# A two-layer encoder trunk on one core: all eight pairs of an MLP part in seven-product form, GpSimd on half of the first product's lower parts, three raw buffers, new token places

## The chip, the cores and the metric

The kernel runs on one core of a Trainium2 chip. A core has a matrix engine (TensorE, PE in the profile, whose weight loads are listed apart as PEld), VectorE (DVE), ScalarE (ACT), GpSimd (POOL) and SyncE (SP, which here only issues transfers). Matmuls write to PSUM; everything else lies in SBUF. The metric is the device time of one execution in microseconds. The kernel before takes 1935.81 us (median of 3 runs, 1935.69 to 1936.0).

## The reference

The input is 256 tokens of width 2048, float32. Layer 0 mixes tokens with a convolution module, layer 1 with multi-head latent attention; each is followed by an MLP with a hidden width of 8192. The MLP is what the change is about:

```python
def sq_relu_mlp(h, w1, w2):
    return jnp.square(jax.nn.relu(h @ w1)) @ w2

for layer in range(DEPTH):
    h = rms_norm(x, norm_mixer_g[layer])
    x = x + (conv_module(h, ...) if layer % N_MIXERS == 0 else mla(h, ...))
    h = rms_norm(x, norm_mlp_g[layer])
    x = x + sq_relu_mlp(h, mlp_w1[layer], mlp_w2[layer])
return rms_norm(x, final_norm_g)
```

`w1` is 2048 x 8192 and `w2` 8192 x 2048 in each layer, 64 MB apiece.

## The kernel before, in words

**Float32 products from parts.** Each float32 operand is split into a higher part `hi` (a rounded copy, made by ScalarE) and a lower part `lo` (the operand minus `hi`, made by VectorE). A product takes three matmuls: hi·hi, lo·hi, hi·lo (`mm3`). The splitting of the weights runs on ScalarE and VectorE all along the kernel, since every weight is used once. `split_into` is the helper of the MLP: one ScalarE copy, then one VectorE subtraction whose two inputs, the raw weights and `hi`, both lie in SBUF.

**The MLP.** The hidden width is cut into 4 parts (q = 0 to 3) of 8 pairs (p = 0 to 7) of 128-wide blocks. The first product ("up", `up_units`) of a pair is made by two units; each loads 1 MB of `w1`, splits it in two halves (h = 0 and 1: one chunk each), and runs 16 matmuls of 512 columns and 16 of 256 columns against the tokens `xt`. After a pair's second unit a list of small steps follows: `add`, `square`, `forms`, `part` (the last splits the hidden values into `sh` and `sl`).

The second product ("down", `down_units`) of a pair with one half of the output width (n2 = 0 or 1) loads 1 MB of `w2`. It comes in two kinds. A plain unit has two chunks of 1024 columns and 24 matmuls of 512 columns. A seven-product unit treats the 2 x 2 blocks of the product in a Strassen-like way: sums of weight blocks (`T`, `V`) are made by VectorE first, four chunks are split (`one` with 512 columns, `two`, `t13` and `t24` with 1024), and 21 matmuls do. It also needs sums of hidden blocks (`forms`). In parts 0 to 2, seven of the eight pairs are of the second kind and pair 2 is plain; in part 3, three pairs (layer 0) or two (layer 1).

**The order of the work** is written out by `stream`. Part 0's up units run alone; then the down units of part q are interleaved with the up units of part q + 1 by the string `ORDERS` (S a seven-product unit, T an up unit, O the plain unit); part 3's down units run alone. So each layer has a first-product stage, three mixed windows and a second-product stage. `stream` splits the weights of the chunk that comes five places later before it issues the matmuls of a chunk (`WB` = 6 buffers of `hi` and of `lo`), and puts one or two of the waiting small steps ahead of each split. Raw weights go through three buffers of the pool `wpool` and a fourth in the MLP's own pool; a buffer is loaded again, by SyncE, once its last reader is done. Hidden values lie in 9 large slots (`N_S`) and 2 smaller ones (`N_G`).

**GpSimd** makes lower parts in the convolution stage (line 171 with the argument `nc.gpsimd`), works on the rotary keys in the attention stage (lines 1267 to 1272 and 1478), and does nothing in the MLPs.

**Places.** Pads of some 32-byte steps (`PAD_O`, `LO_GAP` and others) set where tiles lie. In the up product the lower parts begin 224 bytes into their buffers, so that they lie at 32 bytes modulo 64, while the tokens and `hi` lie at 0 modulo 64.

Of the kernel before, what the change touches and what calls it, by code (L numbers as in the profile page):

```python
# [10 lines left out]
F32 = mybir.dt.float32  # L11
# [7 lines left out]
P = 128  # L19
# [21 lines left out]
LO_GAP = 64  # L41
PAD_STATS = 48
PAD_O = 64
# [13 lines left out]
MADE = tuple((range(8),) * 3 + (last,) for last in ((0, 2, 1, 3, 4, 5, 6, 7),) * 2)  # L57
LATE_G = ((3, 5, 6, 7), (3, 4, 5, 6, 7))
# [25 lines left out]
def trunk_kernel(  # L84
# [231 lines left out]
    def open_xt(name):  # L316
        pool = right_pool(name, 1)
        xt[:] = [
            pool.tile([P, KC // NNB, 2 * S], F32R, name=nm("xt")) for _ in range(NNB)
        ]  # L320

# [3 lines left out]
    open_xt("xt0")  # L325
# [98 lines left out]
    def split_into(parts, src):  # L424
        nc.scalar.activation(parts[0], src, AF.Copy)  # L425
        nc.vector.tensor_tensor(parts[1], src, parts[0].bitcast(F32), op=ALU.subtract)  # L426

    def stream(chunks, todo, blocked, pool):
# [50 lines left out]
    def mlp(layer, ssq, next_gain, finish=None, before=None, last_w1=None):  # L479
# [3 lines left out]
        made_stage, pre, first_tiles, blocked, n_s, sums_left = [], [], {}, {}, [0], []  # L483
# [7 lines left out]
        def up_units(hs, q, p, extra):  # L491
# [3 lines left out]
            large = p in sevens or (q == PARTS - 1 and p in LATE_G[layer])  # L495

            def up_unit(b):
                ps = []

                def chunk(h):  # L500
                    def prep(raw, parts):
                        parts[h] = [a.rearrange("p a (j n) -> p (a j) n", n=P) for a in hi_lo(2, LO_GAP - 8)]
                        split_into(parts[h], raw[:, 8 * h : 8 * h + 8, :])
# [20 lines left out]
                    return Chunk(prep, run, [add, lambda: None, square, forms, part] + extra if b == 1 else [], now=out)  # L524
# [9 lines left out]
            def square():  # L534
                n_s[0] += large
                v = held["u"][:, :, :S]
                nc.scalar.activation(v, v, AF.Relu)
                if p in sevens:
                    held["f"] = f = f_tile()
                    nc.scalar.activation(f[:, 0:4, :].rearrange("p (b t) n -> p b (t n)", b=2), v, AF.Square)  # L540
                    held["src"], shape, tag, n = f[:, 1:8, :], [P, 7, P], "s", N_S
                else:
                    nc.scalar.activation(v, v, AF.Square)
                    held["src"], shape = v, [P, 2, S]
                    tag, n = ("s", N_S) if large else ("g", N_G)
                held["hl"] = [mp.tile(shape, F32R, tag=tag + c, name=nm(tag + c), bufs=n) for c in "hl"]

            def forms():
                if p in sevens:
                    f = held["f"]  # L550
                    nc.vector.tensor_tensor(
                        f[:, 4:6, :], f[:, 0:1, :].broadcast_to([P, 2, P]), f[:, 1:3, :], op=ALU.subtract
                    )
                    nc.vector.tensor_tensor(f[:, 6, :], f[:, 1, :], f[:, 5, :], op=ALU.subtract)
                    nc.vector.tensor_tensor(f[:, 7, :], f[:, 3, :], f[:, 6, :], op=ALU.subtract)

            def part():
                hs[p] = held["hl"]
                split_into(hs[p], held["src"])

            if large:
                blocked[square] = lambda: n_s[0] < N_S and not (p in sevens and sums_left)
            return [up_unit(b) for b in range(2)]

        def down_units(hs, q, n2, held, final):
# [3 lines left out]
            last_plain = max(p for p in range(NPAIR) if p not in sevens)  # L569
# [101 lines left out]
            def seven_unit(p):  # L671
# [80 lines left out]
        with ExitStack() as cx:  # L752
# [46 lines left out]
    with ExitStack() as cx:  # L799
# [389 lines left out]

        ssq, add, prepare = residual_stage(True, g_mlp[0])  # L1190
# [64 lines left out]
    with ExitStack() as cx:  # L1255
# [95 lines left out]

        kvh = at.tile([P, KR // P, S], F32R, name="kvh")
# [435 lines left out]
```

## Time and profile before

| what | value |
|---|---|
| median of 3 runs | 1935.81 us |
| the profiled execution | 1935.74 us |
| its span, first to last instruction | 1933.9 us |
| PE busy | 1910.2 us |
| DVE busy | 1651.6 us |
| ACT busy | 1204.9 us |
| POOL busy | 224.0 us |

Where the stages lie in the span of the profiled execution:

| stage | from | to |
|---|---|---|
| convolution module | 12 | 320 |
| MLP 0: part 0's up units alone | 321 | 409 |
| MLP 0: three mixed windows | 409 | 907 |
| MLP 0: part 3's down units alone | 907 | 982 |
| latent attention | 983 | 1253 |
| MLP 1: up units alone | 1254 | 1342 |
| MLP 1: three mixed windows | 1342 | 1841 |
| MLP 1: down units alone, final norm, output | 1841 | 1934 |

A row of instructions gives the line, the engine, the operation, the tiles written and read, the shape and the count; then busy time, the mean length of one in ns, and the engine's idle time ahead of them. In a row of the timeline the first two numbers are the start and the length in us. Neighbouring instructions of one engine overlap a little in the records (the next begins before the last has ended), so what an instruction costs its engine is the distance from its start to the next start.

### The profile page before, as it was taken

How to read it: one execution, taken by the hardware profiler on the slowest of the kernel's cores; microseconds unless marked ns; L12 is line 12 of the kernel's file. 1: busy time of each engine (PE TensorE's matmuls, PEld its weight loads, DVE VectorE, ACT ScalarE, POOL GpSimd, SP SyncE). 2: the span in 40 equal slices, each digit the busy share in tenths (PEclk: the TensorE clock that was granted, in tenths of full speed). 3: DMA queues.
4: the chain of work that ended last, by engine and by line, in shares of the span. 5: the costliest groups of instructions: out<-in, count | busy, mean ns of one | idle time of the engine just before them, and what ended most of it. 6: DMA issues, size and time to landing. Idle time of an engine off the chain costs nothing.

```text
span 1933.9 us, 28479 instructions
## 1 busy us (share of the span) xinstructions
PE 1910.2 (99%) x10778; PEld 1676.2 (87%) x10778; DVE 1651.6 (85%) x2374; ACT 1204.9 (62%) x1709; POOL 224.0 (12%) x183
## 2 busy tenths in 40 slices
PE   7999999999999999999999999999999999999998
PEld 7999888888888888888899998888888888888886
DVE  5999875789999999999976665657999999999887
ACT  5556664766666666666566665556766666666654
POOL 5999400000000000000001410000000000000000
PEclk9999999999999999999999999999999999999999
DMA  8666456857666667666646445765667766766663
GB/s 235 185 176 176 141 186 174 220 172 208 197 207 204 205 199 212 202 198 215 198 143 181 123 152 175 198 184 174 203 190 210 214 196 195 214 202 197 211 222 109
DMA packets 407113, 367.62 MB, mean 190 GB/s; under 512 B 15416, under 2 KB 351936, under 8 KB 406720
## 3 DMA queue, kind: packets, MB, share of 16 engines
q1 hardware_dynamic: 405952, 363.63, 63.0%
q10 hardware_dynamic: 1024, 2.17, 0.3%
q8 instruction: 84, 1.38, 0.3%
q14 instruction: 53, 0.43, 0.1%
HBM read 363.68 MB, written 2.10 MB: 189 GB/s over the span
## 4 chain that ended last, share of the span: by engine, by line
PE 98%; DVE 1%; DMA 1%; ACT 0%; issue 0%; DVEq 0%; ACTq 0%
PE acc L515 24%; PE acc L196 15%; PE acc L197 15%; PE acc L198 15%; PE acc L513 12%; PE acc L859 3%; PE acc L858 3%; PE acc L860 3%; PE acc L252 1%; PE sum L908 1%; PE acc L1443 0%; PE acc L1445 0%; PE acc L1444 0%; PE acc L1420 0%; PE acc L1421 0%; PE acc L1422 0%
## 5 line engine op out<-in xcount | busy, mean ns | idle before, releaser
L426 DVE TENSOR_TENSOR lo<-raw,hi 128x1024 fp32r<-128x1024 f32 (+1 forms) x512 | 571.8, 1124 | 88.0 <-ACT hi L425 87.7
L425 ACT ACTIVATE hi<-raw 128x1024 fp32r<-128x1024 f32 (+1 forms) x512 | 480.0, 971 | 66.0 <-PE acc L197 65.8
L515 PE MATMUL acc<-xt,hi 128*128 128x512 f32 x2048 | 504.0, 391 | 0.0
L515 PEld LDWEIGHTS acc<-xt,hi 128*128 128x128 f32 x2048 | 374.9, 188 | 72.6
L196 PE MATMUL acc<-hi,sh 128*128 128x512 f32 x930 | 362.7, 390 | 0.0
L198 PE MATMUL acc<-lo,sh 128*128 128x512 f32 x930 | 361.9, 389 | 0.0
L197 PE MATMUL acc<-hi,sl 128*128 128x512 f32 x802 | 312.0, 389 | 0.0
L513 PEld LDWEIGHTS acc<-xt,lo 128*128 128x128 f32 x2048 | 257.7, 188 | 10.9
L513 PE MATMUL acc<-xt,lo 128*128 128x256 f32 x2048 | 259.8, 279 | 0.0
L170 ACT ACTIVATE hi<-raw 128x1024 fp32r<-128x1024 f32 (+2 forms) x184 | 180.0, 1006 | 47.0 <-PE acc L197 42.9
L198 PEld LDWEIGHTS acc<-lo,sh 128*128 128x128 f32 x930 | 174.6, 188 | 36.3
L196 PEld LDWEIGHTS acc<-hi,sh 128*128 128x128 f32 x930 | 174.6, 188 | 35.9
L171 DVE TENSOR_TENSOR lo<-raw,hi 128x1024 fp32r<-128x1024 f32 (+2 forms) x118 | 132.9, 1147 | 68.6 <-ACT hi L170 63.0
L425 ACT ACTIVATE hi<-V 128x1024 fp32r<-128x1024 f32 x94 | 99.6, 1060 | 130.7 <-DVE V L721 123.6
L197 PEld LDWEIGHTS acc<-hi,sl 128*128 128x128 f32 x802 | 150.6, 188 | 31.1
L960 DVE SCALAR_TENSOR_TENSOR sum<-ub,w_dw,sum 128x256 f32<-128x256 f32 x400 | 163.5, 488 | 8.7 <-ACT sum L916 7.0
L171 POOL TENSOR_TENSOR lo<-raw,hi 128x1024 fp32r<-128x1024 f32 x66 | 157.8, 2413 | 24.5 <-ACT hi L170 24.5
L425 ACT ACTIVATE hi<-T 128x1024 fp32r<-128x1024 f32 x94 | 99.5, 1058 | 92.5 <-DVE T L709 69.0
L858 PE MATMUL acc<-xt,hi 128*128 128x256 f32 x512 | 146.3, 286 | 0.0
L859 PE MATMUL acc<-xt,hi 128*128 128x256 f32 x512 | 145.0, 283 | 0.5 <-DVE xt L209 0.5
L860 PE MATMUL acc<-xt,lo 128*128 128x256 f32 x512 | 144.9, 283 | 0.0
L520 ACT ACTIVATE U<-acc 128x512 f32<-128x512 f32 x128 | 75.8, 592 | 108.7 <-PE acc L515 108.6
(270 smaller groups left out, 2808.9 us busy)
## 6 DMA issues: line engine op xcount, KB each, us to landing
raw<-in_mlp_w SPq DMA_DIRECT2D x256, 1024.0 KB, 6.2
raw<-in_conv_w_pw SPq DMA_DIRECT2D x64, 512.0 KB, 5.6
raw<-in_conv_w_pw SPq DMA_DIRECT2D x16, 1024.0 KB, 5.1
raw<-in_mla_w_o SPq DMA_DIRECT2D x16, 1024.0 KB, 5.3
raw<-in_mla_w_kv_up SPq DMA_DIRECT2D x8, 1024.0 KB, 5.4
raw<-in_mla_w_in SPq DMA_DIRECT2D x8, 576.0 KB, 3.8
raw<-in_mla_w_in SPq DMA_DIRECT2D x4, 1024.0 KB, 7.4
raw<-in_mla_w_q_up SPq DMA_DIRECT2D x16, 256.0 KB, 5.0
```

Source lines behind the costliest of these rows:

```text
L170: nc.scalar.activation(hi, raw[:, js, :], AF.Copy)
L171: eng.tensor_tensor(lo, raw[:, js, :], hi.bitcast(F32), op=ALU.subtract)
L196: nc.tensor.matmul(ps, sh, mh, start=start, stop=False)
L197: nc.tensor.matmul(ps, sl, mh, start=False, stop=False)
L198: nc.tensor.matmul(ps, sh, ml, start=False, stop=stop)
L425: nc.scalar.activation(parts[0], src, AF.Copy)
L426: nc.vector.tensor_tensor(parts[1], src, parts[0].bitcast(F32), op=ALU.subtract)
L513: nc.tensor.matmul(ps[0][:, :S], wl[:, j, :], xh(k), start=False, stop=False)
L515: nc.tensor.matmul(ps[0], wh[:, j, :], xhl(k), start=k == 0, stop=k == KC - 1)
L858: nc.tensor.matmul(o, wh[:, bs], xh(k), start=k == 0, stop=False)
L859: nc.tensor.matmul(o, wh[:, bs], xl(k), start=False, stop=False)
L860: nc.tensor.matmul(o, wl[:, bs], xh(k), start=False, stop=k == KC - 1)
```

## The change

Parts 0 to 2 have all eight pairs in seven-product form, so pair 2's plain unit (and the letter O) is gone there; part 3 is as before. In the mixed windows the first half of an order has seven T and the second nine, where there were eight and eight. The hidden values have 11 slots of one size, in the room of the fourth raw buffer and of the two smaller slots. From part 1 on, the lower parts of the second half (h = 1) of each up unit are made by GpSimd. `forms` is cut into three steps (`forms`, `form_2`, `form_4`), which stand only after seven-product pairs. The step `norm`, in part 0, follows pair 2 and no longer the last pair. The tokens of the convolution stage lie 224 bytes lower (at 32 modulo 64), and move to their old place after it; the latents of the attention stage (`kvh` to `qpB`) lie 32 bytes higher.

The diff, without the parts that only move names:

```diff
+PAD_XT = 56
+PAD_KV = 8
-PAD_O = 64
+PAD_O = 56
...
-ORDERS = "STSTSTOSTSTSTSTT", "TSTSTSTOSTSTSTST"
-N_S, N_G = 9, 2
-SEVENS = tuple(((0, 1, 3, 4, 5, 6, 7),) * 3 + (last,) for last in ((0, 2, 4), (0, 2)))
...
+ORDERS = "STSTSTSSTSTSSTT", "TSTSTSTSTSTSTSTST"
+N_S = 11
+SEVENS = tuple((tuple(range(8)),) * 3 + (last,) for last in ((0, 2, 4), (0, 2)))
...
-    def split_into(parts, src):
+    def split_into(parts, src, eng=nc.vector):
         nc.scalar.activation(parts[0], src, AF.Copy)
-        nc.vector.tensor_tensor(parts[1], src, parts[0].bitcast(F32), op=ALU.subtract)
+        eng.tensor_tensor(parts[1], src, parts[0].bitcast(F32), op=ALU.subtract)
...
-        for home in (None, None, None, pool):
+        for home in (None, None, None):
             start(home)
...
-                for _ in range(2 if len(todo) > 4 else 1):
+                for _ in range(2 if len(todo) > 3 else 1):
...
-                        split_into(parts[h], raw[:, 8 * h : 8 * h + 8, :])
+                        split_into(parts[h], raw[:, 8 * h : 8 * h + 8, :], nc.gpsimd if h and q else nc.vector)
...
-                    return Chunk(prep, run, [add, lambda: None, square, forms, part] + extra if b == 1 else [], now=out)
+                    steps = [add, lambda: None, square, *([forms, form_2, form_4] if p in sevens else []), part]
+                    return Chunk(prep, run, steps + extra if b == 1 else [], now=out)
...
-            if large:
-                blocked[square] = lambda: n_s[0] < N_S and not (p in sevens and sums_left)
+            blocked[square] = lambda: n_s[0] < N_S and not (p in sevens and sums_left)
...
                 def close_one():
+                    while forms_left:
+                        todo.pop(0)()
...
-                    for unit in up_units(hs, q, p, [end] if p == MADE[layer][q][-1] and end is not None else [])
+                    for unit in up_units(hs, q, p, [end] if p == (2 if q == 0 else MADE[layer][q][-1]) and end is not None else [])
...
+        open_xt("xt0")
         ssq, add, prepare = residual_stage(True, g_mlp[0])
...
+        at.tile([P, PAD_KV], F32, name="pad_kv")
```

What moves is best seen on two engines. VectorE in layer 0's first mixed window, around the down unit of pair 2 (`lo<-raw` is the lower part of raw weights, with 1024 columns in the up units and in chunk `two`; `T` and `V` are sums of weight blocks, `W` sums of hidden blocks, `sl` the lower part of hidden values), before:

```order
L426 TENSOR_TENSOR lo_4888<-raw_4708,hi_4887 128x1024
L532 TENSOR_TENSOR U_4818<-U_4818 128x2x256
L426 TENSOR_TENSOR lo_4910<-raw_4708,hi_4909 128x1024
L426 TENSOR_TENSOR lo_4924<-raw_4740,hi_4923 128x1024
L551 TENSOR_TENSOR W_4919<-W_4919 128x256
L554 TENSOR_TENSOR W_4919<-W_4919 128x128
L555 TENSOR_TENSOR W_4919<-W_4919 128x128
L426 TENSOR_TENSOR lo_4937<-raw_4740,hi_4936 128x1024
```

An up unit gives two lower parts here (both from `raw_4708`), and the plain unit two (both from `raw_4740`). The same place on VectorE now:

```order
L429 TENSOR_TENSOR lo_4810<-raw_4630,hi_4809 128x1024
L719 TENSOR_TENSOR T_4835<-raw_4731 128x1024
L429 TENSOR_TENSOR lo_4844<-raw_4731,hi_4843 128x512
L726 TENSOR_TENSOR V_4836<-T_4835,raw_4731 128x512
L429 TENSOR_TENSOR lo_4855<-raw_4731,hi_4854 128x1024
L731 TENSOR_TENSOR V_4836<-V_4836,raw_4731 128x512
L429 TENSOR_TENSOR lo_4868<-T_4835,hi_4867 128x1024
L429 TENSOR_TENSOR lo_4878<-V_4836,hi_4877 128x1024
L429 TENSOR_TENSOR lo_4899<-raw_4762,hi_4898 128x1024
```

The up unit on `raw_4630` leaves one lower part on VectorE, and pair 2's unit on `raw_4731` has become a seven-product unit with seven VectorE instructions. GpSimd, from the end of the convolution module on (`lo` at line 171 are its lower parts, `m` and `pad_o` belong to the attention stage), before:

```order
L936 TENSOR_TENSOR tp_2965<-tp_2965,tp_2969 128x256
L171 TENSOR_TENSOR lo_2977<-raw_2632,hi_2976 128x1024
L171 TENSOR_TENSOR lo_2981<-raw_2758,hi_2980 128x1024
L1374 MEMSET pad_o 128x64
L1267 TENSOR_TENSOR m_10690<-scratch,cos 128x128
```

Nothing of layer 0's MLP stands between the convolution and the attention stage there. GpSimd from the same place on, now:

```order
L946 TENSOR_TENSOR tp_2966<-tp_2966,tp_2970 128x256
L172 TENSOR_TENSOR lo_2978<-raw_2633,hi_2977 128x1024
L172 TENSOR_TENSOR lo_2982<-raw_2759,hi_2981 128x1024
L429 TENSOR_TENSOR lo_4725<-raw_4525,hi_4724 128x1024
L429 TENSOR_TENSOR lo_4832<-raw_4630,hi_4831 128x1024
L429 TENSOR_TENSOR lo_4921<-raw_4762,hi_4920 128x1024
L429 TENSOR_TENSOR lo_5064<-raw_4927,hi_5063 128x1024
```

Between the same two stages 48 lower parts have been added, 16 in each mixed window (four are shown; the one on `raw_4630` is the second half of the up unit shown above), and 48 more in layer 1. Over the whole program VectorE's lower parts of 1024 columns from raw weights go from 512 to 404, GpSimd's from 66 to 162, and TensorE's matmuls of 512 columns fall by 36 (3 in each of 12 units).

More of the change, by code (lines that the diff above doesn't have):

```diff
@@ L53 @@
 FILL_AT = (5, 15)
-ORDERS = "STSTSTOSTSTSTSTT", "TSTSTSTOSTSTSTST"
-N_S, N_G = 9, 2
-SEVENS = tuple(((0, 1, 3, 4, 5, 6, 7),) * 3 + (last,) for last in ((0, 2, 4), (0, 2)))
-MADE = tuple((range(8),) * 3 + (last,) for last in ((0, 2, 1, 3, 4, 5, 6, 7),) * 2)
-LATE_G = ((3, 5, 6, 7), (3, 4, 5, 6, 7))
+ORDERS = "STSTSTSSTSTSSTT", "TSTSTSTSTSTSTSTST"
+N_S = 11
+SEVENS = tuple((tuple(range(8)),) * 3 + (last,) for last in ((0, 2, 4), (0, 2)))
+MADE = tuple((range(8),) * 3 + (last,) for last in ((0, 2, 1, 3, 4, 5, 6, 7), (0, 2, 1, 3, 4, 5, 6, 7)))
 N_WARM = 14
@@ L494, in up_units @@
             held = {}
-            large = p in sevens or (q == PARTS - 1 and p in LATE_G[layer])
             def up_unit(b):
@@ L544, in square, with form_2, form_4 @@
                     held["src"], shape = v, [P, 2, S]
-                    tag, n = ("s", N_S) if large else ("g", N_G)
-                held["hl"] = [mp.tile(shape, F32R, tag=tag + c, name=nm(tag + c), bufs=n) for c in "hl"]
+                held["hl"] = [mp.tile(shape, F32R, tag="s" + c, name=nm("s" + c), bufs=N_S) for c in "hl"]
             def forms():
[L549 to L555, printed above, removed]
+                f = held["f"]
+                nc.vector.tensor_tensor(
+                    f[:, 4:6, :], f[:, 0:1, :].broadcast_to([P, 2, P]), f[:, 1:3, :], op=ALU.subtract
+                )
+            def form_2():
+                f = held["f"]
+                nc.vector.tensor_tensor(f[:, 6, :], f[:, 1, :], f[:, 5, :], op=ALU.subtract)
+            def form_4():
+                f = held["f"]
+                nc.vector.tensor_tensor(f[:, 7, :], f[:, 3, :], f[:, 6, :], op=ALU.subtract)
             def part():
+                forms_left.clear()
                 hs[p] = held["hl"]
                 split_into(hs[p], held["src"])
-            if large:
-                blocked[square] = lambda: n_s[0] < N_S and not (p in sevens and sums_left)
+            blocked[square] = lambda: n_s[0] < N_S and not (p in sevens and sums_left)
             return [up_unit(b) for b in range(2)]
@@ L568, in down_units @@
             last_seven = max(sevens)
-            last_plain = max(p for p in range(NPAIR) if p not in sevens)
+            last_plain = max((p for p in range(NPAIR) if p not in sevens), default=None)
             last = q == PARTS - 1
```

13 lines of the change are left out of this document (8 added, 5 removed).

## The prediction

> **What bounds the kernel now.** I read the page's busy times and its chain first, then the stages of an MLP one by one.
>
> ```profile
> PE 1910.2 (99%) x10778; PEld 1676.2 (87%) x10778; DVE 1651.6 (85%) x2374; ACT 1204.9 (62%) x1709; POOL 224.0 (12%) x183
> PE 98%; DVE 1%; DMA 1%; ACT 0%; issue 0%; DVEq 0%; ACTq 0%
> ```
>
> TensorE bounds the whole, so fewer matmuls would shorten it, as long as nothing else is nearly as full. Whether something is, the average does not tell. The next view has layer 0's up units alone, its mixed windows, its down units alone, and layer 1's mixed windows; the columns after the times are PE, PEld, DVE, ACT and POOL busy.
>
> ```profile
> 320.00:409.00 89.00, 89.00 (x519) 78.46 (x520) 64.87 (x100) 55.42 (x79) 0.00 (x0) 1.00 0.66 185
> 409.00:907.00 498.00, 498.00 (x2565) 426.55 (x2564) 473.91 (x551) 330.24 (x401) 0.00 (x0) 1.00 0.67 202
> 907.00:983.00 76.00, 76.00 (x341) 63.07 (x340) 70.63 (x80) 43.17 (x50) 0.15 (x1) 1.00 0.56 183
> 1342.00:1841.00 499.00, 499.00 (x2569) 427.39 (x2568) 473.87 (x549) 330.08 (x402) 0.00 (x0) 1.00 0.68 202
> ```
>
> In the mixed windows, where all of the change to the MLP lies, DVE works 473.9 of 498 us. It has 24 us to spare per layer, 8 in each window. There a seven-product unit trades TensorE time for DVE time, and GpSimd is to pay for it. The question is what a GpSimd instruction costs DVE.
>
> **What GpSimd costs.** In the MLPs GpSimd is idle, so the prices are from elsewhere. The lower parts in the convolution stage give its duration, and the attention stage shows it beside VectorE's lower parts from raw weights, the same operation as in the MLP (two inputs in SBUF):
>
> ```profile
> L171 POOL TENSOR_TENSOR lo<-raw,hi 128x1024 fp32r<-128x1024 f32 x66 | 157.8, 2413 | 24.5 <-ACT hi L170 24.5
> ...
> 1057.45 0.47 POOL L1268 TENSOR_TENSOR m<-scratch,sin 128x128 f32<-128x128 f32 x1
> 1057.88 0.46 POOL L1269 TENSOR_TENSOR m<-scratch,cos 128x128 f32<-128x128 f32 x1
> 1058.30 1.44 POOL L1270 TENSOR_TENSOR m<-scratch,sin 128x128 f32<-128x128 f32 x1
> 1059.70 1.44 POOL L1271 TENSOR_TENSOR qp<-m,m 128x128 f32<-128x128 f32 x1
> 1061.10 0.97 POOL L1272 TENSOR_TENSOR qp<-m,m 128x128 f32<-128x128 f32 x1
> 1083.95 0.74 POOL L1478 TENSOR_TENSOR qhl<-qp,qhl 128x256 fp32r<-128x256 f32 x1 [2.95 <-ACT qhl L202]
> ```
>
> ```profile
> 1057.93 2.89 DVE L171 TENSOR_TENSOR lo<-raw,hi 128x1024 fp32r<-128x1024 f32 x2 [1.76 <-ACT hi L170]
> 1060.74 0.41 DVE L207 TENSOR_TENSOR qTl<-acc,qTh 128x256 fp32r<-128x256 f32 x1
> 1061.08 0.68 DVE L171 TENSOR_TENSOR lo<-raw,hi 128x512 fp32r<-128x512 f32 x1
> 1084.42 0.81 DVE L171 TENSOR_TENSOR lo<-raw,hi 128x512 fp32r<-128x512 f32 x1 [1.48 <-ACT hi L170]
> ```
>
> The same GpSimd instruction takes 0.46 us alone, and 0.97 or 1.44 where a lower part of VectorE is running: the one at 1061.10 ends 0.31 us after that lower part does (1061.08 + 0.68 = 1061.76, against 1062.07). It has waited for the end. And it goes the other way: the lower part at 1084.42 starts 0.27 us before the GpSimd instruction ends (1084.69), and takes 0.81 us in place of 0.68. So the two take turns, each whole, and GpSimd lets go some 0.14 us before its record ends (0.27 - 0.13). By that a GpSimd lower part of 1024 columns keeps VectorE out for 2413 - 140 = 2270 ns; by the slope between 128 and 1024 columns ((2413 - 460) / 896 = 2.18 ns a column) for 2230. I take 2.24 us. An instruction with an input in PSUM (`qTl<-acc`, 0.41 us beside GpSimd's 1.44) is not held up.
>
> The Trainium skill, "SBUF — State Buffer", section "Who interferes with whom", states the same rule: a VectorE instruction with two SBUF inputs and a GpSimd instruction that reads SBUF exclude each other, for the whole instruction. By "whole" the hold would be 2.41 us, and the sum below 16 us longer; the trace's 0.14 us decide for the shorter one.
>
> What VectorE pays for its own instructions is read from start to start, in an up unit and a seven-product unit of layer 0:
>
> ```profile
> 600.90 0.42 DVE L551 TENSOR_TENSOR W<-W 128x256 f32<-128x256 f32 x1
> 601.35 0.29 DVE L554 TENSOR_TENSOR W<-W 128x128 f32<-128x128 f32 x1
> 601.68 0.29 DVE L555 TENSOR_TENSOR W<-W 128x128 f32<-128x128 f32 x1
> 601.89 1.22 DVE L426 TENSOR_TENSOR lo<-raw,hi 128x1024 fp32r<-128x1024 f32 x1
> 603.03 1.22 DVE L709 TENSOR_TENSOR T<-raw 128x1024 f32<-128x1024 f32 x1
> 604.16 1.08 DVE L426 TENSOR_TENSOR sl<-W,sh 128x896 fp32r<-128x896 f32 x1
> 605.16 0.69 DVE L426 TENSOR_TENSOR lo<-raw,hi 128x512 fp32r<-128x512 f32 x1
> 605.76 0.69 DVE L716 TENSOR_TENSOR V<-T,raw 128x512 f32<-128x512 f32 x1
> 606.37 1.22 DVE L426 TENSOR_TENSOR lo<-raw,hi 128x1024 fp32r<-128x1024 f32 x1
> 607.50 0.69 DVE L721 TENSOR_TENSOR V<-V,raw 128x512 f32<-128x512 f32 x1
> 608.11 1.22 DVE L426 TENSOR_TENSOR lo<-T,hi 128x1024 fp32r<-128x1024 f32 x1
> 609.32 1.23 DVE L426 TENSOR_TENSOR lo<-V,hi 128x1024 fp32r<-128x1024 f32 x1
> 610.46 1.22 DVE L426 TENSOR_TENSOR lo<-raw,hi 128x1024 fp32r<-128x1024 f32 x1
> ```
>
> 1024 columns cost 1.14 us (601.89 to 603.03), 512 columns 0.60, `sl` 1.00, the three `W` together 0.99.
>
> **The change part by part, for one layer's three mixed windows.**
>
> *Lower parts to GpSimd:* 16 per window, 48 x 1.14 = 54.7 us less on VectorE.
>
> *Seven-product form for pair 2:* six plain units go, with 12 x 1.14 = 13.7 us of lower parts; also three lower parts of hidden values (0.6 each, 1.8) and six additions to the residual (0.67 each by their 0.75 us below, 4.0). Six seven-product units come, each 1.13 + 0.60 + 0.61 + 1.13 + 0.61 + 1.14 + 1.14 = 6.36 us: 38.2; and three times `W` and `sl`, 6.0. VectorE's own work is then 473.9 - 74.2 + 44.2 = 443.9 us.
>
> *GpSimd's turns:* 48 x 2.24 = 107.5 us, in which VectorE's next instruction, nearly always one with two SBUF inputs, stands still. Together 551.4 us have to pass one after the other, where the window lasts 498. TensorE then waits for lower parts, and the port that VectorE and GpSimd share becomes the bound: 53 us over.
>
> Three corrections. VectorE enters the mixed windows five chunks ahead, and may use that lead up: one up chunk and four of a seven-product unit, 1.14 + 6.36, about 8 us off. The instructions that read PSUM can run beside GpSimd:
>
> ```profile
> L583 DVE SCALAR_TENSOR_TENSOR xs<-acc,r,xs 128x512 f32<-128x512 f32 x18 | 13.2, 746 | 0.2
> L603 DVE TENSOR_TENSOR W<-W,acc 128x512 f32<-128x512 f32 x3 | 2.1, 688 | 0.1
> ```
>
> With the other three groups like the second (12 instructions) and six of the first gone, that is 12 x 0.67 + 12 x 0.61 = 15 us, of which GpSimd's share of the time (107 of 551, a fifth) meets 3. I take 2 us off, and add 2 for the restart of the down units without a lead and for what VectorE still waits for ScalarE. That gives 551.4 - 8 = 543, or 45 us over per layer, and 90 us for both.
>
> *Fewer matmuls:* 36 of 512 columns. They start 0.227 us apart:
>
> ```profile
> 600.15 0.39 PE L197 MATMUL acc<-hi,sl 128*128 128x512 f32 x1
> 600.38 0.39 PE L198 MATMUL acc<-lo,sh 128*128 128x512 f32 x1
> 600.60 1.98 PE L515 MATMUL acc<-xt,hi 128*128 128x512 f32 x8
> 602.42 2.03 PE L513 MATMUL acc<-xt,lo 128*128 128x256 f32 x16
> 604.29 2.00 PE L515 MATMUL acc<-xt,hi 128*128 128x512 f32 x8
> ```
>
> That is 8.2 us, all in windows where TensorE is no longer the bound: nothing, while the port is. If the port were not, they would count in full.
>
> *New places:* the 16 matmuls of 256 columns above, whose weights lie at 32 modulo 64 and whose tokens at 0, start 0.117 us apart (602.42 to 604.29). The change gives the convolution stage (1536 matmuls of that size in the program) and parts of the attention stage (672) such a distance. There, now:
>
> ```profile
> 80.00:200.00 120.00, 120.00 (x1004) 120.00 (x1004) 119.47 (x309) 69.17 (x117) 112.57 (x75) 1.00 0.64 177
> ```
>
> They take 120 ns each (120 us by 1004), so at best 3 ns x 1536 = 4.6 and 3 x 672 = 2.0 us. But the up units' matmuls next to the low ones lose a part of it again (the eight of 604.29, up to the next at 606.13, take 1.84 us against 1.82 for those of 600.60), so the other end is a small loss, 2 us. And VectorE is busy 119.47 of 120 us in the convolution stage: a faster TensorE finds it late next. I take 1.5 us of gain for both stages.
>
> *Three raw buffers:* a load lands in 6.2 us.
>
> ```profile
> raw<-in_mlp_w SPq DMA_DIRECT2D x256, 1024.0 KB, 6.2
> ```
>
> An up unit and a seven-product unit will last some 11 us together (543 by 48), so a ring of three turns in 17; landing and the reading of a unit (about 6) leave 4 to spare. Nothing, unless GpSimd holds a buffer much longer. SyncE's queue has only these loads in it.
>
> *Small steps:* `forms` in three pieces issues the same instructions; `norm` moves to a place where VectorE works 64.9 of 89 us; the 11 slots and the longer first order shift which unit stands where, not how many. Nothing.
>
> The sum is made against the profiled execution (1935.74 us, 1.84 of it outside the span, and 0.07 below the median): 1935.7 + 90 - 1.5 = 2024 us.
>
> **Rivals.**
>
> *The exclusion does not bind (faster).* If a GpSimd lower part kept VectorE out for little, TensorE would stay the bound: 1935.7 - 8.2 - 1.5 = 1926 us. The point that decides: VectorE's 443.9 us leave 498 - 4 + 8 - 443.9 = 58 us per layer, or 1.2 us for each of the 48. For it speaks only that in the convolution stage GpSimd is busy 112.6 of 120 us beside a VectorE at 119.5; but VectorE's taps there have one input in PSUM. Against it speak all the rows of the attention stage above.
>
> *Half of the hold is hidden* in VectorE's waits and PSUM reads, 1.6 us left: 443.9 + 76.8 - 8 - 498 = 15 us per layer, 1964 us.
>
> *VectorE keeps its waits* of 24 us per layer for ScalarE on top: 2024 + 48 = 2072 us. For it: those waits are short ones for `hi`, once per pair. Against it: they fall where VectorE is five chunks ahead, which it will not be.
>
> *The ring of three binds:* GpSimd's part comes last on its raw buffer, so that each reload is late by a microsecond: 96 of them, 2120 us. Against it: the 4 us to spare.
>
> **How the numbers follow.** The sum: 0.66, for 2005 to 2050. Waits kept: 0.12. Half hidden: 0.08. Ring: 0.06. No exclusion: 0.08, nearly all of it faster. A measurement of this kernel tells 0.2% (4 us) from no change. The range goes from 1985 (all 15 us of PSUM reads hidden, the lead a little longer, the places' full gain: 551.4 - 15 - 10 - 498 = 28 per layer, less 6.6) to 2085, which takes in the kept waits and leaves out the half, the ring and the faster case.
>
> **What would show it.** In the mixed windows of the changed kernel: TensorE's matmuls with idle time ended by DVE and POOL; DVE near full, its lower parts beside GpSimd at some 3.4 us (1.14 + 2.24) against 1.22; POOL's longer than 2.4 because they wait; each layer's windows about 540 us in place of 498; the other stages as they are. I would be wrong if VectorE's instructions kept 1.22 us beside GpSimd, or if SyncE's loads ended TensorE's waits.

## The result, and the profile after

The changed kernel takes 2005.82 us (median of 4 runs, 2004.3 to 2005.87) against 1935.87 us (4 runs, 1935.69 to 1936.0) for the kernel before on the same chip: a ratio of 1.036, 95% interval 1.0342 to 1.0377. The forecast was 2024, slower, with a range from 1985 to 2085.

The page of the changed kernel, its busy times and its chain:

```profile
PE 1931.8 (96%) x10742; PEld 1659.3 (83%) x10742; DVE 1760.3 (88%) x2344; ACT 1220.9 (61%) x1733; POOL 519.0 (26%) x279
PE 50%; DVE 20%; issue 10%; ACT 7%; POOL 7%; DMA 5%; POOLq 0%; ACTq 0%; DVEq 0%
```

The chain, 98% TensorE before, now runs through TensorE for half of the span; most of the rest is VectorE, ScalarE and GpSimd. The stages show where. The next view of the changed kernel has layer 0's and layer 1's mixed windows; the columns are as in the prediction.

```profile
407.80:942.30 534.50, 511.11 (x2546) 420.78 (x2545) 526.13 (x525) 334.95 (x411) 147.81 (x49) 1.00 0.62 186
...
1376.90:1910.50 533.60, 511.00 (x2545) 420.64 (x2544) 524.93 (x522) 334.58 (x410) 147.62 (x48) 1.00 0.62 187
```

VectorE is busy 526.1 of 534.5 us there. Measured from the first `acc<-hi,sh` of a layer to its last `acc<-xt`, the mixed windows last 534.3 and 533.5 us, where both lasted 497.6: +36.7 and +35.9. What lies ahead of them is 1.7 us shorter (they begin at 407.65, before at 409.32), the attention part between them 0.9 us (434.8 against 435.7), and the end has not moved (93.7 us). These add up to the 70.1 us by which the span grew (1933.9 to 2004.0).

What TensorE waits for in layer 0's mixed windows (total us, times, longest):

```profile
PE acc L515 <- POOL lo L429: 11.5, 15, 1.2
PE acc L199 <- DVE lo L429: 10.5, 26, 0.8
```

And one turn of GpSimd, on VectorE and on GpSimd of the changed kernel:

```profile
503.38 0.69 DVE L535 TENSOR_TENSOR U<-U 128x512 f32<-128x512 f32 x1
503.98 3.39 DVE L719 TENSOR_TENSOR T<-raw 128x1024 f32<-128x1024 f32 x1
507.30 0.68 DVE L429 TENSOR_TENSOR lo<-raw,hi 128x512 fp32r<-128x512 f32 x1
```

```profile
503.36 2.93 POOL L429 TENSOR_TENSOR lo<-raw,hi 128x1024 fp32r<-128x1024 f32 x1 [14.10 <-ACT hi L428]
...
L429 POOL TENSOR_TENSOR lo<-raw,hi 128x1024 fp32r<-128x1024 f32 x96 | 295.3, 3081 | 1162.9 <-ACT hi L428 981.7 <-PE acc L199 156.5 <-PE acc L198 24.7
```

GpSimd starts at 503.36, and its 2.93 us are 0.52 longer than the 2.41 of such an instruction in the convolution stage: it waits for `U<-U`. `T<-raw` (1.22 us before) starts at 503.98, waits for GpSimd in its turn, and takes 3.39. Its 3.39 - 1.22 = 2.17 us are what the turn cost.

### The profile page after: what moved, and what is told of

Same layout as the page of the kernel before. It is cut to its first block, busy times and chain, and to the rows that moved or that the text cites. A ratio compares the mean times of both kernels' runs of the same rounds, so it can differ in the third digit from the quotient of the medians.

```text
span 2004.0 us, 28620 instructions
## 1 busy us (share of the span) xinstructions
PE 1931.8 (96%) x10742; PEld 1659.3 (83%) x10742; DVE 1760.3 (88%) x2344; ACT 1220.9 (61%) x1733; POOL 519.0 (26%) x279
## 3 DMA queue, kind: packets, MB, share of 16 engines
q10 hardware_dynamic: 1024, 2.17, 0.3%
## 4 chain that ended last, share of the span: by engine, by line
PE 50%; DVE 20%; issue 10%; ACT 7%; POOL 7%; DMA 5%; POOLq 0%; ACTq 0%; DVEq 0%
PE acc L517 11%; PE acc L197 9%; PE acc L199 9%; PE acc L198 9%; POOL lo L429 7%; DVE sum L970 6%; PE acc L515 6%; ACT hi L428 5%; DMA raw<-in_mlp_w 4%; DVE lo L429 3%; DVE T L719 3%; DVE V L731 1%; DVE V L726 1%; DVE U L535 1%; DVE xs L591 1%
## 5 line engine op out<-in xcount | busy, mean ns | idle before, releaser
L429 POOL TENSOR_TENSOR lo<-raw,hi 128x1024 fp32r<-128x1024 f32 x96 | 295.3, 3081 | 1162.9 <-ACT hi L428 981.7
L429 DVE TENSOR_TENSOR lo<-raw,hi 128x1024 fp32r<-128x1024 f32 (+1 forms) x416 | 517.8, 1248 | 46.0 <-ACT hi L428 46.0
L199 PE MATMUL acc<-lo,sh 128*128 128x512 f32 x1046 | 416.9, 399 | 23.1 <-DVE lo L429 20.7
L197 PE MATMUL acc<-hi,sh 128*128 128x512 f32 x1046 | 408.7, 391 | 0.0
L198 PE MATMUL acc<-hi,sl 128*128 128x512 f32 x918 | 357.9, 390 | 0.0
L515 PE MATMUL acc<-xt,lo 128*128 128x256 f32 x2048 | 269.6, 281 | 22.9 <-POOL lo L429 22.5
L199 PEld LDWEIGHTS acc<-lo,sh 128*128 128x128 f32 x1046 | 196.2, 188 | 98.0 <-DVE lo L429 59.2
L719 DVE TENSOR_TENSOR T<-raw 128x1024 f32<-128x1024 f32 x106 | 230.7, 2177 | 0.0
L197 PEld LDWEIGHTS acc<-hi,sh 128*128 128x128 f32 x1046 | 196.5, 188 | 37.5
L198 PEld LDWEIGHTS acc<-hi,sl 128*128 128x128 f32 x918 | 172.4, 188 | 36.0
L172 POOL TENSOR_TENSOR lo<-raw,hi 128x1024 fp32r<-128x1024 f32 x66 | 157.6, 2409 | 24.2 <-ACT hi L171 24.2
```

The costliest lines, as they stand in the source:

```text
L172: eng.tensor_tensor(lo, raw[:, js, :], hi.bitcast(F32), op=ALU.subtract)
L197: nc.tensor.matmul(ps, sh, mh, start=start, stop=False)
L198: nc.tensor.matmul(ps, sl, mh, start=False, stop=False)
L199: nc.tensor.matmul(ps, sh, ml, start=False, stop=stop)
L429: eng.tensor_tensor(parts[1], src, parts[0].bitcast(F32), op=ALU.subtract)
L515: nc.tensor.matmul(ps[0][:, :S], wl[:, j, :], xh(k), start=False, stop=False)
```

## The experiments

The theory (1): a lower part on GpSimd costs VectorE its whole turn, some 2.2 us in place of the 1.14 us that it took from VectorE, and VectorE becomes the bound. A rival (2): the time comes from the rest of the change (the seven-product form, the slots, the order), or from TensorE's waits for single late parts, which VectorE's load does not tell.

### All lower parts back on VectorE

```diff
-                        split_into(parts[h], raw[:, 8 * h : 8 * h + 8, :], nc.gpsimd if h and q else nc.vector)
+                        split_into(parts[h], raw[:, 8 * h : 8 * h + 8, :], nc.vector)
```

> The changed kernel with all lower parts of the first product back on VectorE. Theory 1 (GpSimd and VectorE take turns, 2.2 us for each GpSimd lower part): the loss of 70 us goes. VectorE's own work in the three mixed windows is 443.9 + 54.7 = 498.6 us per layer, less some 8 of lead, plus some 8 of waits, against TensorE's 494: about 1926 to 1940 us. Theory 2 (the eighth seven-product pair, the smaller ring or the new order cost the time, not GpSimd): it stays near 2000 us, or rises, since VectorE has more to do.

1936.42 us (11 runs), ratio 1.0 (0.9991 to 1.0009). So moving these lower parts to GpSimd makes 69.4 of the 70 us, and what else the change does is worth nothing in sum as long as VectorE makes them: the new places gain about as much as the two layers' mixed windows lose (1.7 us each). Layer 0's mixed windows of this run:

```profile
407.80:907.30 499.50, 497.60 (x2546) 422.14 (x2545) 492.48 (x575) 337.14 (x412) 0.14 (x1) 1.00 0.68 202
```

VectorE has only 7 us left. The 18 matmuls that a layer saves (4.1 us) do not show, for the window is 499.3 us and not 493.5: by the starts of its matmuls, TensorE now loses 5.2 us per layer in 24 short waits of 0.1 to 0.5 us, which it did not have before. The profile names what ended the six longest (1.4 us): lower parts of VectorE.

### GpSimd alone, in the kernel before

```diff
-    def split_into(parts, src):
+    def split_into(parts, src, eng=nc.vector):
         nc.scalar.activation(parts[0], src, AF.Copy)
-        nc.vector.tensor_tensor(parts[1], src, parts[0].bitcast(F32), op=ALU.subtract)
+        eng.tensor_tensor(parts[1], src, parts[0].bitcast(F32), op=ALU.subtract)
...
-                        split_into(parts[h], raw[:, 8 * h : 8 * h + 8, :])
+                        split_into(parts[h], raw[:, 8 * h : 8 * h + 8, :], nc.gpsimd if h and q else nc.vector)
```

> The kernel before with only one edit: GpSimd makes half of the first product's lower parts, from part 1 on. Theory 1: VectorE's own work falls to 473.9 - 54.7 = 419.2 us per layer, GpSimd's turns add 48 x 2.2 = 106 of which some 14 hide at the closings as in the changed kernel, waits 8, lead -8: about 512 against 498, 1936 + 27 = 1963 us (1945 to 1975). Theory 2: no loss, 1936 us, since VectorE has 55 us less to do per layer.

2058.46 us (5 runs, 2054.07 to 2066.71), ratio 1.0642 (1.062 to 1.0664): slower, as expected, but by 123 us and not by 27. Theory 1 as it stood is not enough here. Layer 0's mixed windows of this run, and TensorE's waits there:

```profile
409.10:974.70 565.60, 525.84 (x2566) 445.00 (x2565) 496.89 (x504) 328.00 (x401) 195.47 (x48) 0.95 0.58 177
```

```profile
PE acc L513 <- POOL lo L426: 38.3, 14, 4.4
```

VectorE is busy 496.9 of 565.6 us, so it is not the bound. TensorE waits for lower parts of GpSimd, 14 times and up to 4.4 us; and its granted clock, 1.00 before, is 0.95, so that the same matmuls take 525.8 us in place of 498.0. The two make the window: 38.3 + 27.8 = 66 of its 67.6 us. One of these places, on GpSimd, VectorE and TensorE:

```profile
583.48 8.16 POOL L426 TENSOR_TENSOR lo<-raw,hi 128x1024 fp32r<-128x1024 f32 x1 [8.69 <-ACT hi L425]
```

```profile
583.00 1.22 DVE L426 TENSOR_TENSOR lo<-raw,hi 128x1024 fp32r<-128x1024 f32 x1
584.14 1.22 DVE L709 TENSOR_TENSOR T<-raw 128x1024 f32<-128x1024 f32 x1
585.27 0.69 DVE L426 TENSOR_TENSOR lo<-raw,hi 128x512 fp32r<-128x512 f32 x1
585.88 0.69 DVE L716 TENSOR_TENSOR V<-T,raw 128x512 f32<-128x512 f32 x1
586.48 1.22 DVE L426 TENSOR_TENSOR lo<-raw,hi 128x1024 fp32r<-128x1024 f32 x1
587.61 0.69 DVE L721 TENSOR_TENSOR V<-V,raw 128x512 f32<-128x512 f32 x1
588.22 1.22 DVE L426 TENSOR_TENSOR lo<-T,hi 128x1024 fp32r<-128x1024 f32 x1
589.50 3.22 DVE L426 TENSOR_TENSOR lo<-V,hi 128x1024 fp32r<-128x1024 f32 x1
```

```profile
591.70 2.08 PE L513 MATMUL acc<-xt,lo 128*128 128x256 f32 x8 [4.38 <-POOL lo L426]
```

GpSimd's part is there from 583.48, and six instructions of VectorE, each with its inputs in SBUF, start after that and are not held up. Each starts before the one ahead has ended. Only where VectorE pauses (`lo<-T,hi` ends at 589.44, `lo<-V,hi` starts at 589.50) does GpSimd get its turn; it ends at 591.64, and TensorE has waited 4.38 us. In this kernel 11 of layer 0's 48 parts were passed in that way, by six or seven instructions; in the changed kernel none by more than three, and 37 by none. So the turns are not taken in the order of arrival, and a part can be late even where VectorE has time. Moving the same lower parts costs 123 us in this kernel and 69 in the changed one, so there the rest of the change does count; which piece of it keeps GpSimd's parts from being passed, no run shows.

### Three raw buffers alone, and the places alone

Each is one part of the change, made in the kernel before.

```diff
-        for home in (None, None, None, pool):
+        for home in (None, None, None):
```

> The kernel before with three raw buffers in place of four and nothing else. Theory 1: a load lands in 6.2 us and a ring of three turns in about 15.5, so nothing is seen: 1934 to 1938 us. Theory 2 (the ring binds): matmuls wait for parts whose loads are late, 1945 us or more.

1935.79 us (11 runs), ratio 1.0 (0.9991 to 1.0009): the fourth buffer was not needed.

```diff
-PAD_O = 64
+PAD_XT = 56
+PAD_KV = 8
+PAD_O = 56
...
-    open_xt("xt0")
+    open_xt("xtc", PAD_XT)
...
+        open_xt("xt0")
         ssq, add, prepare = residual_stage(True, g_mlp[0])
...
+        at.tile([P, PAD_KV], F32, name="pad_kv")
```

> The kernel before with only the new token places (the convolution stage's tokens and the attention stage's latents). From the two profiles: the stage up to the MLP ends 1.7 us earlier in the changed kernel, the attention stage is 1.0 us shorter. Theory 1 (the places do this): 1933 us. Rival: these were effects of the MLP's other state at the stage's ends, and the places do nothing: 1936 us.

1933.04 us (11 runs, 1931.5 to 1933.35), ratio 0.9983 (0.9974 to 0.9991): 2.7 us faster; that is 0.14%, less than the 0.2% of the prediction, but the interval of these many runs lies below 1. It has the lowest median here. The convolution stage of the changed kernel, which has these places too:

```profile
80.00:200.00 120.00, 120.00 (x1031) 120.00 (x1031) 120.00 (x311) 71.87 (x125) 114.07 (x73) 1.00 0.67 185
```

1031 matmuls in the 120 us where 1004 were: 116.4 ns each in place of 119.5. VectorE, at 119.47 before, is at 120.00.

A part of the gain is lost again at the end of that stage, where TensorE waits for a tile of VectorE, `ub`. The kernel before, this run, and the run of the next experiment, which has these places too:

```profile
209.79 5.02 PE L908 MATMUL sum<-ub,dg 128*128 128x256 f32 x22 [1.15 <-DVE ub L883]
206.29 6.67 PE L912 MATMUL sum<-ub,dg 128*128 128x256 f32 x22 [2.04 <-DVE ub L887]
206.45 5.02 PE L922 MATMUL sum<-ub,dg 128*128 128x256 f32 x22 [2.06 <-DVE ub L897]
```

With the new places `ub` comes 3.5 us earlier (206.29 against 209.79), and TensorE is ready for it 4.4 us earlier, so that it waits 0.9 us longer. In the second row TensorE's granted clock then falls to 0.50 for 3.4 us, and the same 22 matmuls take 1.7 us longer; in the third it stays at 1.00. Six of the eight profiled executions with these places show this fall, the changed kernel's too, behind a wait of 2.03 us; in the kernel before, it is not there. The 11 times of this run lie at 1931.5 to 1931.6 us (five) and 1933.0 to 1933.4 (six, the profiled one among them), that is 4.2 or 2.6 us below the kernel before; that the fall parts them also where no profile was taken is inferred from their distance. So a difference of less than 1.7 us between two medians of kernels with these places can come from this alone.

### An unread subtraction on GpSimd

With all lower parts on VectorE, GpSimd does work that nobody waits for.

```diff
-                        split_into(parts[h], raw[:, 8 * h : 8 * h + 8, :], nc.gpsimd if h and q else nc.vector)
+                        split_into(parts[h], raw[:, 8 * h : 8 * h + 8, :])
+                        if h and q:
+                            src = parts[h][0].rearrange("p a n -> p (a n)")[:, :NB].bitcast(F32)
+                            dm = mp.tile([P, NB], F32, tag="dm", name=nm("dm"), bufs=1)
+                            nc.gpsimd.tensor_tensor(dm, src, src, op=ALU.subtract)
```

> All lower parts are on VectorE again (1936.4 us without more); in the changed kernel's 48 places per layer GpSimd subtracts 512 columns of the same higher part from themselves, into a tile that nobody reads. So no engine waits for GpSimd's result; only the port is used. Theory 1 (GpSimd and VectorE take turns, and the time of GpSimd's instruction is what VectorE loses): by the slope of 2.18 ns a column one of these instructions lasts 460 + 384 x 2.18 = 1300 ns and keeps VectorE out for 1.16 us; 48 x 1.16 = 56 us, of which 84 per cent meet it (89.0 of 105.5 in the changed kernel), 47; VectorE had 7 us to spare: 40 to 49 us per layer more, 2016 to 2034 us. Theory 2 (what costs is that TensorE waits for lower parts that come late from GpSimd, and VectorE could stand the turns): 1936 to 1945 us.

1999.74 us (4 runs, 1998.26 to 2000.61), ratio 1.033 (1.0316 to 1.0344). Theory 2 falls: no engine needs this result, and the kernel is 63 us slower than without it. The size was expected 16 us too high at the least. Its mixed windows, and one place on VectorE (GpSimd's instruction starts at 502.75):

```profile
406.10:938.10 532.00, 511.40 (x2546) 417.90 (x2545) 526.16 (x572) 335.96 (x410) 93.92 (x49) 1.00 0.63 188
...
502.76 0.68 DVE L539 TENSOR_TENSOR U<-U 128x512 f32<-128x512 f32 x1
503.37 2.06 DVE L429 TENSOR_TENSOR lo<-raw,hi 128x1024 fp32r<-128x1024 f32 x1
```

2.06 - 1.22 = 0.84 us is what a turn cost, not 1.16, and VectorE, which makes all lower parts itself here, is again full (526.2 of 532.0 us).

### Zeros written by GpSimd

```diff
-                        split_into(parts[h], raw[:, 8 * h : 8 * h + 8, :], nc.gpsimd if h and q else nc.vector)
+                        if h and q:
+                            nc.gpsimd.memset(parts[h][1].rearrange("p a n -> p (a n)").bitcast(F32), 0.0)
+                        split_into(parts[h], raw[:, 8 * h : 8 * h + 8, :])
```

> All lower parts are on VectorE (1936.4 us without more); in the 48 places per layer GpSimd writes zeros to the 1024 columns of the buffer before VectorE writes the lower part there. GpSimd reads nothing. Theory 1a (it is GpSimd's reading of two inputs that excludes VectorE): 1934 to 1942 us, VectorE's lower parts keep 1.22 us. Theory 1b (any access of GpSimd to SBUF takes the port): by the 132 ns for 30 columns in the convolution stage, a time for 1024 columns of 0.9 to 1.2 us is estimated, 48 x 1 x 0.84 = 40 us per layer less 7 to spare: 2000 us, with VectorE's lower parts at some 2.2 us.

1937.1 us (10 runs), ratio 1.0004 (0.9995 to 1.0013): theory 1a. GpSimd's instructions of this run:

```profile
L506 POOL MEMSET lo<- 128x1024 f32 x96 | 91.7, 956 | 1281.9 <-PE acc L517 1043.3 <-PE acc L199 210.6 <-DVE W L565 18.7
```

VectorE's lower parts of raw weights in layer 0's mixed windows, all of which it makes here:

```profile
L429 DVE TENSOR_TENSOR lo<-raw,hi 128x1024 fp32r<-128x1024 f32 x144 | 174.8, 1221 | 2.3 <-ACT hi L428 1.9
```

96 memsets, 0.96 us each, and VectorE's lower parts keep 1.22 us (1215 to 1231 ns), though every memset in these windows lies beside VectorE instructions with two SBUF inputs. It is GpSimd's reading that collides.

### GpSimd only at the closings, and everywhere else

In the middle of each mixed window, where the sums of half a part are closed, three up units stand in a row (two T at the end of the first string of `ORDERS`, one at the head of the second). There VectorE has residual additions that read PSUM. VectorE in the changed kernel at the first of these places, and GpSimd:

```profile
479.06 1.22 DVE L429 TENSOR_TENSOR lo<-raw,hi 128x1024 fp32r<-128x1024 f32 x1
481.24 2.39 DVE L429 TENSOR_TENSOR lo<-raw,hi 128x1024 fp32r<-128x1024 f32 x1 [0.96 <-ACT hi L428]
483.55 1.40 DVE L591 SCALAR_TENSOR_TENSOR xs<-acc,r,xs 128x512 f32<-128x512 f32 x2
484.87 2.12 DVE L429 TENSOR_TENSOR lo<-raw,hi 128x1024 fp32r<-128x1024 f32 x1
486.91 0.74 DVE L591 SCALAR_TENSOR_TENSOR xs<-acc,r,xs 128x512 f32<-128x512 f32 x1
```

```profile
479.85 9.41 POOL L429 TENSOR_TENSOR lo<-raw,hi 128x1024 fp32r<-128x1024 f32 x3 [15.30 <-ACT hi L428]
```

Three turns, and only the two lower parts are longer, by 1.17 and 0.90 us: 2.07 in place of 3 x 2.2. Two kernels divide the places.

```diff
-                        split_into(parts[h], raw[:, 8 * h : 8 * h + 8, :], nc.gpsimd if h and q else nc.vector)
+                        split_into(parts[h], raw[:, 8 * h : 8 * h + 8, :], nc.gpsimd if h and q and 2 * MADE[layer][q].index(p) + b in (5, 6, 7) else nc.vector)
```

> GpSimd makes only the lower parts of the three up units that stand in a row at the middle of each mixed window: 9 per layer in place of 48. Theory 1 (in the changed kernel these three turns meet additions that read PSUM, and cost VectorE 2.07 us together, where a VectorE lower part costs 1.14 each): VectorE has 9 x 1.14 - 3 x 2.07 = 4.0 us per layer less to do than with all lower parts on it, where it bounds the mixed windows at 499.4 us: 495 to 496, and 1928 to 1930 us. Theory 2 (each turn costs about the same, 2.2 us, wherever it stands): 9 x (2.2 - 1.14) = 9.5 us per layer more, of which some 2 lie in VectorE's idle time: 1946 to 1956 us.

The other has `not in` for `in`:

> The opposite: GpSimd makes the second halves' lower parts of all up units but the three in a row of each window, 39 per layer; these 9 are VectorE's again. So GpSimd has a fifth less to do. Theory 1 (these nine turns were nearly hidden): VectorE gets 9 x 1.14 = 10.3 us and loses 3 x 2.07 = 6.2 us of turns: 4 us per layer more, 2012 to 2016 us, slower than the changed kernel. Theory 2 (all turns cost alike, 89.0 / 48 = 1.85 us): 9 x (1.85 - 1.14) = 6.4 us per layer less, 1991 to 1995 us.

Only at the closings: 1934.01 us (11 runs, 1933.86 to 1935.76), ratio 0.9995 (0.9986 to 1.0003). Everywhere else: 2007.24 us (4 runs), ratio 1.0369 (1.0353 to 1.0385). Layer 0's mixed windows of the one, and of the other:

```profile
407.80:906.70 498.90, 497.19 (x2546) 422.15 (x2545) 488.69 (x566) 337.10 (x412) 28.22 (x10) 1.00 0.67 202
```

```profile
407.80:943.10 535.30, 511.66 (x2545) 420.74 (x2545) 529.90 (x534) 334.89 (x410) 119.62 (x40) 1.00 0.62 186
```

Theory 2 of both falls: with a fifth less on GpSimd the kernel is not faster (+1.4 us), and the nine turns at the closings cost no more than the work that they take off VectorE. But theory 1's steps were too large both times, by 4 to 6 and by 5 to 9 us. The times of both kernels part in two as those of the places alone do; set side by side, the first takes 0.9 us less than the kernel with all lower parts on VectorE (1935.7 against 1936.6 us, and 1933.9 against 1934.8), where some 8 were expected. Taking the length of each VectorE instruction less its median in the kernel before, the turns cost VectorE 84.0 us in 39 places (2.15 each) and 5.8 us in the nine, as expected; the difference went into VectorE's idle time, most of it waits for ScalarE (10.2 us idle in the first, where all lower parts on VectorE left 7.0; 5.4 in the second, 8.4 in the changed kernel). In the first, TensorE's short waits (4.5 and 4.9 us in the two layers) lie mostly where the run without GpSimd has them, from 445 to 473 and at 528 for instance, away from the places that became lighter.

### GpSimd's parts in two pieces

This asks why the unread subtraction was cheap.

```diff
-        eng.tensor_tensor(parts[1], src, parts[0].bitcast(F32), op=ALU.subtract)
+        n = src.shape[1]
+        for c in ((slice(0, n // 2), slice(n // 2, n)) if eng is nc.gpsimd else (slice(0, n),)):
+            eng.tensor_tensor(parts[1][:, c, :], src[:, c, :], parts[0][:, c, :].bitcast(F32), op=ALU.subtract)
```

> The changed kernel, with each of GpSimd's lower parts of the MLPs made by two instructions of 512 columns in place of one of 1024. In the run with the unread subtractions a turn of 512 columns cost VectorE 0.845 us, where one of 1024 columns costs 2.20: less than half. Theory 1 (that is the price of a shorter instruction): two turns cost 1.69 us, 0.51 us less in each of the 43 places per layer that cost in full: 22 us per layer less, 1955 to 1970 us. Theory 2 (the unread subtraction was cheap since its two inputs are the same tile; the time goes by the columns read): two turns cost 2.2 to 2.4 us, 2004 to 2025 us. In both, a turn of VectorE may come between the two, so that the lower part is ready later; if TensorE waits for that, it comes on top.

2003.47 us (4 runs, 2001.64 to 2003.83), ratio 1.0347 (1.0332 to 1.0363): theory 2, half a microsecond below its range. VectorE in the changed kernel so altered:

```profile
501.25 2.33 DVE L721 TENSOR_TENSOR T<-raw 128x1024 f32<-128x1024 f32 x1
503.50 1.76 DVE L431 TENSOR_TENSOR lo<-raw,hi 128x512 fp32r<-128x512 f32 x1
505.18 0.68 DVE L728 TENSOR_TENSOR V<-T,raw 128x512 f32<-128x512 f32 x1
```

`T<-raw` is 1.11 us longer and the lower part 1.07: two turns, with one instruction of VectorE between them, and together the 2.2 us of one turn of 1024 columns. So the price goes by the columns, 2.15 ns each, and has no fixed part that shows. A shorter instruction is not what made the unread subtraction cheap; its two inputs were the same tile, which is the likely reason, but it also wrote another tile, and no run has the one without the other.

The same in the kernel before, with GpSimd alone added (the 75.9 us named in the expectation are those of both layers; layer 0 has 38.3):

> The kernel before with GpSimd on half of the lower parts (2058.46 us in one instruction), here with two instructions of 512 columns each. Theory 1 (its cost beyond VectorE's work comes from single GpSimd parts that VectorE's instructions pass, so that TensorE waits for them): two instructions have to get in twice, the part is later still: 2058 to 2120 us, with TensorE's waits for GpSimd above the 75.9 us of layer 0. Theory 2 (the cost is the length of the turn): shorter turns, 2015 to 2050 us.

2069.36 us (4 runs, 2063.51 to 2073.26), ratio 1.0696 (1.0678 to 1.0714): in theory 1's range, with a median 11 us above the one with whole parts, though the runs of the two overlap (that one's reach from 2054.07 to 2066.71). TensorE's waits in the whole of this run, and of the one with whole parts:

```profile
PE acc L515 <- POOL lo L428: 75.4, 49, 3.3
```

```profile
PE acc L513 <- POOL lo L426: 75.9, 28, 4.4
```

They have not grown in sum, as theory 1 had it; they are more and shorter. These two executions took 2063.51 and 2065.28 us, so the traces cannot show where the 11 us between the medians lie, and theory 1 is not shown; theory 2 falls by the time.

## Why the prediction was right, and where its sizes were off

**The bound and its cause: right.** The port that VectorE and GpSimd share became the bound of the mixed windows, VectorE's instructions beside GpSimd took 3.4 us in place of 1.22, TensorE waited for both, and the rest of the program stayed as it was but for the 2.6 us of the new places. The run with all lower parts on VectorE shows that GpSimd is the cause, and the unread subtraction that a GpSimd instruction takes VectorE's time even where nobody waits for its result. In the changed kernel half of TensorE's waits end with a part of GpSimd (11.5 of 22.0 us); that these are late because VectorE is full, and not for a reason of their own as in the kernel with GpSimd alone, is argued from VectorE's 526.1 of 534.5 us.

**The sum: 45 us per layer forecast, 36.7 and 35.9 measured.** Term by term, for layer 0:

| term of the sum | forecast | measured |
|---|---|---|
| VectorE's own work, less the lead | 443.9 - 8 = 435.9 | 437.1 (526.1 busy - 89.0 lost) |
| GpSimd's turns, less what PSUM reads hide | 107.5 - 2 = 105.5 | 89.0 |
| what VectorE waits besides | 2 | 8.4 |
| the window | 543 | 534.5 |

The term that was mis-sized is GpSimd's turns. Its price was near: 2.15 us for 2.24. What failed is the step "of which GpSimd's share of the time (107 of 551, a fifth) meets 3", on the 15 us of instructions that read PSUM. It took them as spread evenly, but the order puts nine of the 48 turns at the closings, where these instructions are: six turns beside them, and the first of each three in part in a wait of VectorE for ScalarE (0.96 us in the place shown). Some 12 of the 17 us of PSUM-reading instructions lie within GpSimd's records, and the nine turns cost 5 to 6 us in place of 20: the two kernels that divide the places show it. By the forecast's own rows the places could have been told: the three T in a row are in the diff, and the bound of 15 us was in the text. The difference (16.5) is 39 x 0.09 = 3.5 for the price and 13 for the place. VectorE's waits, 6.4 us more than forecast, gave some of it back.

**Fewer matmuls: nothing, right.** That they "would count in full" if the port were not the bound is not shown. With all lower parts on VectorE the port is not the bound, and they do not count; but there VectorE itself is at 492.5 of 499.5 us and late by tenths of a microsecond in 24 places per layer. What they would be worth with VectorE at the 443.9 us of the first rival, no run shows.

**New places: 1.5 us forecast, 2.7 measured** alone, within the 6.6 and the loss of 2 that were its ends. That a faster TensorE "finds it late next", VectorE, is what happened: TensorE's wait at the end of the stage grew from 1.15 to 2.04 us, and the fall of the clock behind it, which the forecast did not have, takes 1.7 us in some executions. **Three raw buffers and the small steps: nothing**, right; the first was measured alone.

**The rivals.** No exclusion falls by VectorE's 3.39 us. Half of the hold hidden: a sixth at most was (89.0 of 107.5 remain, and a part of that is the price). VectorE's waits kept: 8.4 of 24 us were. The ring of three falls by its own run, and in the changed kernel's windows none of TensorE's waits that the profile lists ends with a load.

**The rule of the Trainium skill**, "SBUF — State Buffer", section "Who interferes with whom", on VectorE instructions with two SBUF inputs and GpSimd instructions that read SBUF: these runs agree in both directions, since the parts that read cost 2.15 us a turn and the zeros that only write left VectorE's instructions at their length. That the hold lasts "for the whole instruction", which the section says of VectorE's two-port modes and the prediction took over, holds here only roughly: 2.15 to 2.20 us of a record of 2.41.

## What to carry to other kernels

Moving a subtraction with two SBUF inputs from VectorE to GpSimd does not relieve VectorE where its next instruction also has two SBUF inputs: here it took 1.14 us off and put 2.15 us on. What cost next to nothing here was a part beside VectorE instructions that read PSUM (nine per layer), and GpSimd work that only writes (a memset); look at what VectorE does in those very microseconds, not at its share of the whole. And sum the engines' loads only as a lower bound: a GpSimd part can be late by several microseconds where VectorE never pauses, and an engine at 98% gives a gain elsewhere back in waits of tenths of a microsecond.

## What the runs showed of the hardware that was not expected

- GpSimd's turn does not come in the order of arrival. In the kernel before with GpSimd added, 11 of 48 parts waited while six or seven VectorE instructions, each starting before the last had ended, went past; in the changed kernel 37 of 48 were not passed at all. What decides it is not settled; in the place shown, GpSimd got in when VectorE paused for 0.06 us.
- A late part can cost more than its wait, since TensorE's clock can fall after it. In the run with GpSimd alone, the 4.3 us after the wait of 4.38 us, and the 5 us after those:

```profile
591.70:596.00 4.30, 4.30 (x14) 3.82 (x15) 2.17 (x2) 0.00 (x0) 0.00 (x0) 0.50 0.60 166
596.00:601.00 5.00, 5.00 (x23) 4.04 (x23) 2.72 (x3) 4.14 (x6) 2.54 (x1) 0.98 0.78 273
```

  The granted clock (third number from the end) is 0.50, then nearly full again. In the changed kernel, after the longest wait of its mixed windows, 1.24 us, it stays at 1.00:

```profile
506.30:511.00 4.70, 4.65 (x24) 4.03 (x25) 4.70 (x6) 2.81 (x4) 0.00 (x0) 1.00 0.70 220
```

  Of the run with GpSimd alone, 28 us in layer 0 and 22 in layer 1 (TensorE busy 520.3 us in place of 498.0) are the clock. The Trainium skill, "TensorE: Matmul & The Clock Gate", section "What's actually happening", puts the point at an idle window of some 3.4 us, and the state after it at half clock; the 0.50 agrees, the point does not. In the run with two pieces in the kernel before, the clock is 0.68 from 477.7 to 483 us, behind a wait of 2.50 us and with one of 1.47 us in it; in the changed kernel it is 0.50 from 207 to 210 us, behind 2.03 us, and in the changed kernel with two pieces from 505.5 to 508.5 us, behind 1.48 us; yet behind 2.06 us in the run with the unread subtraction it stays at 1.00. What decides it was not followed.
- A GpSimd subtraction of 512 columns kept VectorE out for 1.10 us with two different inputs, and for 0.84 us with one tile as both.
- With the tokens moved from 0 to 32 modulo 64 bytes and the weights left in place, the convolution stage's 256-column matmuls start 116.4 ns apart in place of 119.5.
